# Attention scores on one core: the first unit loaded contiguously and stored in halves of 64 partitions, PSUM in groups of two, three and three banks

## The chip, the core and the metric

The kernel runs on one core of a Trainium2 chip. The metric is the device time in microseconds, the median of several runs. Six names recur. PE is the matrix engine, PEld its loading of weights. DVE is the vector engine, ACT the scalar engine, POOL the general engine GpSimd, and SP the engine that issues most DMAs and waits for their semaphores. All DMAs of a core, whoever issues them, run on its 16 DMA engines.

## The reference

For each of 8 batches and 8 heads, the scores of 512 queries against 512 keys of 64 numbers are computed and scaled. There is no softmax, so the output is much larger than the inputs: 67.1 MB of float32 against twice 8.4 MB.

```python
# q, k: (8, 8, 512, 64) float32
scale = 1.0 / np.sqrt(q.shape[-1])
return (np.einsum('bhqd,bhkd->bhqk', q, k) * scale).astype(np.float32)
```

## The kernel before

**Units and tiles.** The work is cut into 4 units of two batches each (index `v`), and the output into 16 tiles of 4 MB (index `g`), four for each unit. A tile holds four heads: two (`x`) lie one behind the other in each partition, and two (`h`) in partitions 0 to 63 and 64 to 127. A partition holds 8 rows (`i`) of 512 scores for each `x`. Two successive tiles belong to the same batch `b`.

**Loads.** `rows(v, x)` gives the DRAM view of the keys (`x` = 0) or queries (`x` = 1) of one unit: 128 partitions of 16 KB, in the order (s h m) (b x), where the head number is split as (x s h). This order makes the two heads in the halves of a tile neighbours in DRAM, so that a whole tile is one regular pattern over 128 partitions (`out_r`). The loads go to the three large buffers `bigs`, which later hold the tiles on their way out. The keys of unit 0 are loaded in four parts by `load_part` (line 78): part `n` fills every fourth partition, 32 partitions in all, 512 KB. Part 0 goes out on SP's queue and part 1 on ACT's before the program's first barrier, parts 2 and 3 on SP after it. The other loads are 2 MB each, on SP (`load`, line 70). The last two wait until unit 1 has been cast, since they reuse its buffer.

**Cast and transpose.** POOL casts each load to bf16 into `xb` (line 131), in two instructions per load, and counts `ready`. For unit 0's keys it waits for all four parts first. DVE then transposes 32x32 blocks: for each batch two instructions for the keys into `kT` (`turn_keys`, line 162) and four for the queries into `qz` (`turn_queries`, line 170). `qz` is zeroed once (line 185), so that one matmul handles two heads: the rows that belong to the other head are zero. The transposes of the next batch are put in between the evacuations of the present one, at places that a table fixes:

```python
after = {(0, 1): 1, (0, 4): 1, (0, 6): 2, (1, 1): 2}
```

**Matmuls and PSUM.** PE runs 16 matmuls of 128x512 per tile (line 152), in a hardware loop over four tiles. PSUM has 8 banks, used as four tensors `pss` of two banks. A pair of matmuls fills one of them; PE waits until the pair four places earlier has been read.

**Evacuation.** Each pair is scaled and moved to the tile's buffer by ACT (line 202) or DVE (line 205), one instruction of 128x1024 each, in an order written out by hand:

```python
takers = ["act", "dve", "act", "act", "dve", "act", "dve", "act"]
```

So a tile takes five instructions on ACT and three on DVE. Each one counts a semaphore `act0`, `act1`, `dve0` or `dve1` (by batch, alternating).

**Stores and buffers.** SP waits until both counters say that tile `g` is complete (line 102), issues its store as one DMA (line 103), and then waits until the buffer of tile `g + 2` is free: until the store that used it has landed, or, at the start, until POOL has cast what was loaded there (line 112). It then counts `next0` or `next1`, for which PE waits before it begins that tile. Everything on SP is in this one order. After the last store it waits for all stores to land (line 114).

Of the kernel before, what the change touches and what calls it, by code (L numbers as in the profile page):

```python
# [5 lines left out]
def kernel(  # L6
# [5 lines left out]
    nc = tc.nc  # L12
    B, H, S, D = q.shape
    scale = 1.0 / (D ** 0.5)
    P = 128
    Q = 32
    UNITS = B // 2
    G = H // 2
    M = P // (2 * H)
    R = S // M  # L20
    J = R // 2
    RO = 8
    U = S // RO
    JJ = J // RO
    PAIRS = RO
    ALL = 2 * B

    f32 = mybir.dt.float32
    bf16 = mybir.dt.bfloat16
    mult = mybir.AluOpType.mult  # L30
# [3 lines left out]
    names = ["ready", "zeroed", "pe", "next0", "next1", "act0", "act1", "dve0", "dve1"]  # L34
    sem = {name: nc.alloc_semaphore(name) for name in names}
    load_sems = [nc.alloc_semaphore(f"load{n}") for n in range(2 * UNITS)]
    parts = [load_sems[0]] + [nc.alloc_semaphore(f"load0_{n}") for n in range(1, 4)]
    store_sems = [nc.alloc_semaphore(f"store{n}") for n in range(3)]

    q_r = q.rearrange("(v b) (x s h) (m j) d -> v (s h m) (b x) (j d)", b=2, x=2, s=2, j=R)
    k_r = k.rearrange("(v b) (x s h) (m j) d -> v (s h m) (b x) (j d)", b=2, x=2, s=2, j=R)
    out_r = out.rearrange("(v b) (x s h) (u i) k -> v s b (h u) x (i k)", b=2, x=2, s=2, i=RO)

    bigs = [nc.alloc_sbuf_tensor(f"big{n}", [P, 2, RO, S], f32)[:] for n in range(3)]
    xb = nc.alloc_sbuf_tensor("xb", [P, 2 * UNITS, J, D, 2], bf16)[:]
    kT = nc.alloc_sbuf_tensor("kT", [P, 2 * G, S], bf16)[:]
    qz = nc.alloc_sbuf_tensor("qz", [P, 2 * G, RO, P], bf16)[:]
    pss = [nc.alloc_psum_tensor(f"ps{n}", [P, 2, S], f32)[:] for n in range(4)]  # L50

    xw = xb.rearrange("p n w d e -> p n (w d e)").bitcast(f32).rearrange(
        "p n (w d) -> p n w d", d=D)
# [5 lines left out]
    def xf(v):  # L59
        return bigs[(0, 1, 2, 1)[v]].rearrange("p x i k -> p (x i k)").rearrange(  # L60
            "p (x s c) -> p x s c", x=2, s=2)

    def store_buffer(g):
        return bigs[(0, 2, 1)[g % 3]]

    def rows(v, x):
        return (k_r, q_r)[x][v]

    def load(v, x):
        nc.sync.dma_start(out=xf(v)[:, x].rearrange("p s c -> p (s c)"), in_=rows(v, x)  # L70
                          ).then_inc(load_sems[2 * v + x], 16)

    def load_part(queue, n):
        dst = xf(0)[:, 0].rearrange("p s c -> p (s c)")[n:P:4]
        return queue.dma_start(out=dst, in_=rows(0, 0)[:, n]).then_inc(parts[n], 16)  # L78

    for n, queue in enumerate((nc.sync, nc.scalar)):  # L80
        tc.no_tile_sem_insts.add(load_part(queue, n).ins.name)
    tc.close()
    tc.compile()  # L83

    takers = ["act", "dve", "act", "act", "dve", "act", "dve", "act"]
    share = {who: takers.count(who) for who in ("act", "dve")}
    taken = [takers[:p + 1].count(takers[p]) for p in range(PAIRS)]


    for n in (2, 3):
        load_part(nc.sync, n)
    for n in range(1, 2 * (UNITS - 1)):
        load(n // 2, n % 2)
    nc.sync.sem_inc(sem["next0"], 1)
# [3 lines left out]
    for g in range(ALL):  # L100
        for who in ("act", "dve"):
            nc.sync.wait_ge(sem[f"{who}{g // 2 % 2}"], share[who] * (g % 2 + 1))
        nc.sync.dma_start(out=out_r[g // 4, g // 2 % 2, g % 2],
                          in_=store_buffer(g).rearrange("p x i k -> p x (i k)")
                          ).then_inc(store_sems[g % 3], 16)
        for later in ((1, 2) if g == 0 else (g + 2,)):
            if later < ALL:
                if later < 3:
                    nc.sync.wait_ge(sem["ready"], 4 + 2 * later)
                else:  # L110
                    nc.sync.wait_ge(store_sems[later % 3], later // 3 * 16)
                nc.sync.sem_inc(sem[f"next{later // 2 % 2}"], 1)  # L112
    for n in range(3):
        nc.sync.wait_ge(store_sems[n], 16 * len(range(n, ALL, 3)))


    for v in range(UNITS):
        for x in range(2):
            for part in [load_sems[2 * v + x]] if v or x else parts:
                nc.gpsimd.wait_ge(part, 16)  # L120
            for s in range(2):
                src = xf(v)[:, x, s]
                dst = xb[:, 2 * v + x]
                if x == 0:
                    src = src.rearrange("p (w e d) -> p w e d", e=2, d=D)
                    dst = dst[:, s * J // 2:(s + 1) * J // 2].rearrange("p w d e -> p w e d")
                else:
                    src = src.rearrange("p (jj e i d) -> p jj e i d", e=2, i=RO, d=D)
                    dst = dst.rearrange("p (i jj) d e -> p jj e i d", i=RO)[
                        :, s * JJ // 2:(s + 1) * JJ // 2]  # L130
                cast = nc.gpsimd.tensor_copy(out=dst, in_=src)  # L131
            cast.then_inc(sem["ready"], 1)

    pe = nc.tensor
    pe.wait_ge(sem["zeroed"], 2)
    with pe.Fori(0, ALL // 4):
        for t in range(4):
            two, r = divmod(t, 2)  # L140
            off = {1: ("act", 2 * share["act"]), 2: ("dve", 2 * share["dve"]), 3: ("next", 2)}
            for p in range(PAIRS):
                n, i = t * 2 + p // 4, p % 4 * 2
                ahead = (p + 4) % PAIRS
                of = t if p >= 4 else (t + 3) % 4
                for w in range(2):
                    if w == 0:
                        who = takers[ahead]
                        pe.wait_ge(sem[f"{who}{of // 2}"], of % 2 * share[who] + taken[ahead])
                    elif p == 0:  # L150
                        pe.wait_ge(sem[f"next{two}"], r + 1)
                    ins = pe.matmul(out=pss[p % 4][:, w, :], lhsT=qz[:, n, i + w], rhs=kT[:, n],  # L152
                                    start=True, stop=True)
                    if w == 0 and r == 1 and p in off:
                        ins.then_inc(sem[f"{off[p][0]}{1 - two}"], -off[p][1])
                ins.then_inc(sem["pe"], 1)

    def turn_keys(b, y):  # L160
        s = b % 2 * 2 * Q
        return nc.vector.transpose(  # L162
            out=kw[2 * y * Q:2 * (y + 1) * Q, b % 2 * G:(b % 2 + 1) * G].rearrange(
                "d g (m w) -> d w m g", w=J),
            in_=xw[s:s + 2 * Q, b // 2 * 2, :, y * Q:(y + 1) * Q])

    def turn_queries(b, y, h):
        s = (b % 2 * 2 + h) * Q
        d = (2 * y + h) * Q
        return nc.vector.transpose(  # L170
            out=qw[d:d + Q, b % 2 * G:(b % 2 + 1) * G, :, h * Q:(h + 1) * Q].rearrange(
                "d g i (m jj) -> d i jj m g", jj=JJ),
            in_=xw[s:s + Q, b // 2 * 2 + 1, :, y * Q:(y + 1) * Q].rearrange(
                "p (i jj) d -> p i jj d", i=RO))

    def steps(b):
        nc.vector.wait_ge(sem["ready"], b // 2 * 2 + 1)
        yield turn_keys(b, 0)
        yield turn_keys(b, 1)
        nc.vector.wait_ge(sem["ready"], b // 2 * 2 + 2)  # L180
        for y in range(2):
            for h in range(2):
                yield turn_queries(b, y, h)
# [7 lines left out]
    last.then_inc(sem["zeroed"], 1)  # L191


    after = {(0, 1): 1, (0, 4): 1, (0, 6): 2, (1, 1): 2}
    coming = iter(())
    for pair in range(ALL * PAIRS):
        g, p = divmod(pair, PAIRS)
        o = store_buffer(g)[:, p // 4, p % 4 * 2:p % 4 * 2 + 2, :]
        ps = pss[pair % 4]
        if takers[p] == "act":  # L200
            nc.scalar.wait_ge(sem["pe"], pair + 1)
            freed = nc.scalar.mul(out=o, in_=ps, mul=scale)  # L202
        else:
            nc.vector.wait_ge(sem["pe"], pair + 1)
            freed = nc.vector.tensor_scalar(out=o, in0=ps, scalar1=scale, scalar2=None, op0=mult)  # L205
        freed.then_inc(sem[f"{takers[p]}{g // 2 % 2}"], 1)
        if p == 0 and g % 2 == 0 and g // 2 + 1 < 2 * UNITS:
            coming = steps(g // 2 + 1)
        for _ in range(after.get((g % 2, p), 0)):
            next(coming, None)  # L210


# [28 lines left out]
```

## Time and profile before

| | |
|---|---|
| median of 3 runs | 201.52 us (201.32 to 201.67) |
| the profiled execution: time, span | 201.43 us, 200.1 us |
| DMA | 83.90 MB (read 16.78, written 67.11), mean 419 GB/s |
| DVE busy | 154.9 us (77%), 97 instructions |
| ACT busy | 79.5 us (40%), 81 instructions |
| PE busy | 85.8 us (43%) |
| POOL busy | 39.0 us (19%), 20 instructions |
| granted PE clock, mean | 0.773 |

The span runs from the first to the last instruction of the profiled execution; the 1.3 us between it and the time lie around it. Busy times are sums over a whole span with different stages in it. An engine can be busy for most of a span and still not set its end, if its work is finished before somebody needs it; and DMA engines have no line of their own in the list of busy times but a row in tenths per slice of the span.

### The profile page before, as it was taken

The page shows a single profiled execution, that of the slowest core. Times are in us where ns is not written, and L with a number is a line of the kernel's source. Part 1 is how long each engine was busy: PE and PEld are TensorE (multiplying, and loading weights), DVE is VectorE, ACT ScalarE, POOL GpSimd, SP SyncE. Part 2 cuts the span into 40 slices and gives each one's busy share as a digit, 9 for nine tenths or more (in the row PEclk, how much of TensorE's full clock was granted, in tenths as well). Part 3 has the DMA queues.
Part 4 walks back from the last instruction along what each step waited for, and adds up shares of the span by engine and source line. Part 5 has one row for each costly group of instructions (what it writes and reads, how often), then busy time and mean ns, then how long its engine had stood idle before and what let it go on. Part 6 is the DMA issues. An engine that isn't in the chain of part 4 may idle for free.

```text
span 200.1 us, 839 instructions
## 1 busy us (share of the span) xinstructions
PE 85.8 (43%) x252; PEld 27.5 (14%) x256; DVE 154.9 (77%) x97; ACT 79.5 (40%) x81; POOL 39.0 (19%) x20
## 2 busy tenths in 40 slices
PE   0000056294844483547236822754575357910000
PEld 0000021121211121112112211211121112300000
DVE  3317959997999899999998999899989996830000
ACT  2000027163752485248443843383437345840000
POOL 0199999996000000000000000000000000000000
PEclk9999999757875588587975799696559667995555
DMA  5999999999999999999999999999999999999996
GB/s 213 380 432 419 432 439 436 423 406 439 429 429 429 436 429 431 426 436 436 429 426 431 436 432 429 429 432 432 429 436 429 432 429 429 426 429 426 436 432 265
DMA packets 5554, 83.90 MB, mean 419 GB/s; under 512 B 432, under 2 KB 432, under 8 KB 432
## 3 DMA queue, kind: packets, MB, share of 16 engines
q1 hardware_dynamic: 5504, 83.36, 97.9%
q10 hardware_dynamic: 48, 0.52, 0.7%
q14 instruction: 2, 0.02, 0.0%
HBM read 16.78 MB, written 67.11 MB: 419 GB/s over the span
## 4 chain that ended last, share of the span: by engine, by line
DVE 54%; DMA 11%; POOL 10%; PE 6%; ACT 3%; SPq 2%; issue 1%
DVE qz L170 24%; DVE big L205 19%; DVE kT L162 12%; DMA big<-in_k_dram 11%; POOL xb L131 10%; PE ps L152 6%; ACT big L202 3%; SPq L70 2%; SPq L78 1%; SPq L112 0%
## 5 line engine op out<-in xcount | busy, mean ns | idle before, releaser
L152 PE MATMUL ps<-kT,qz 128*128 128x512 bf16 x252 | 85.8, 496 | 90.4 <-DVE big L205 57.0
L202 ACT ACTIVATE big<-ps 128x1024 f32<-128x1024 f32 x80 | 78.2, 1025 | 95.4 <-PE ps L152 95.4
L170 DVE STREAM_TRANSPOSE qz<-xb 32x1024 f32<-32x1024 f32 x32 | 64.1, 2004 | 1.5 <-POOL xb L131 1.0
L205 DVE TENSOR_SCALAR big<-ps 128x1024 f32<-128x1024 f32 x48 | 57.8, 1219 | 9.3 <-PE ps L152 8.9
L152 PEld LDWEIGHTS ps<-kT,qz 128*128 128x128 bf16 x256 | 27.5, 118 | 148.3 <-issue 71.6
L131 POOL CAST xb<-big 128x2048 bf16<-128x2048 f32 x16 | 38.8, 2472 | 9.0 <-DMA big<-in_k_dram 8.7
L162 DVE STREAM_TRANSPOSE kT<-xb 64x1024 f32<-64x1024 f32 x16 | 31.1, 1944 | 7.6 <-POOL xb L131 7.1
L185 DVE MEMSET qz<- 128x4096 uint32 x1 | 3.5, 3472 | 3.5 <-PEq L83 3.5
L202 ACT ACT_TABLE_LOAD x1 | 1.3, 1283 | 2.6 <-PEq L83 2.6
L225 POOL MEMSET const-float32-0.0<- 128x1 f32 x1 | 0.1, 99 | 0.2 <-issue 0.2
L225 POOL MEMSET const-bfloat16-1.0<- 128x1 bf16 x1 | 0.1, 102 | 0.0
L225 POOL MEMSET const-uint8-127<- 128x1 uint8 x1 | 0.1, 102 | 0.0
L225 POOL MEMSET const-float32-1.0<- 128x1 f32 x1 | 0.1, 99 | 0.0
## 6 DMA issues: line engine op xcount, KB each, us to landing
out_dram<-big SPq DMA_DIRECT2D x16, 4096.0 KB, 15.0
big<-in_q_dram SPq DMA_DIRECT2D x4, 2048.0 KB, 16.0
big<-in_k_dram SPq DMA_DIRECT2D x3, 2048.0 KB, 14.7
big<-in_k_dram SPq DMA_DIRECT2D x3, 512.0 KB, 5.2
big<-in_k_dram ACTq DMA_DIRECT2D x1, 512.0 KB, 5.7
```

Source lines behind the costliest of these rows:

```text
L70: nc.sync.dma_start(out=xf(v)[:, x].rearrange("p s c -> p (s c)"), in_=rows(v, x)).then_inc(load_sems[2 * v + x], 16)
L78: return queue.dma_start(out=dst, in_=rows(0, 0)[:, n]).then_inc(parts[n], 16)
L131: cast = nc.gpsimd.tensor_copy(out=dst, in_=src)
L152: ins = pe.matmul(out=pss[p % 4][:, w, :], lhsT=qz[:, n, i + w], rhs=kT[:, n], start=True, stop=True)
L162: return nc.vector.transpose(out=kw[2 * y * Q:2 * (y + 1) * Q, b % 2 * G:(b % 2 + 1) * G].rearrange("d g (m w) -> d w m g", w=J), in_=xw[s ...
L170: return nc.vector.transpose(out=qw[d:d + Q, b % 2 * G:(b % 2 + 1) * G, :, h * Q:(h + 1) * Q].rearrange("d g i (m jj) -> d i jj m g", jj=J ...
L185: nc.vector.memset(qz, 0.0).then_inc(sem["zeroed"], 1)
L202: freed = nc.scalar.mul(out=o, in_=ps, mul=scale)
L205: freed = nc.vector.tensor_scalar(out=o, in0=ps, scalar1=scale, scalar2=None, op0=mult)
L225: nc = _bacc.Bacc("TRN2", target_bir_lowering=False, num_devices=1)
```

## The change

Two things change together.

*Unit 0.* The keys and queries of the first two batches are loaded in DRAM order: partition (b, g, m), 16 KB each, 2 MB in one stretch. The first load, of the keys, is cut by columns instead of partitions: two DMAs of 128 partitions with 8 KB each, one on SP's queue and one on ACT's (semaphores `halves`). POOL waits for each half ahead of the cast that reads it. With this order the two heads in the halves of a tile are no longer neighbours but four heads apart, so each of the tiles 0 to 3 is stored by two DMAs, one from partitions 0 to 63 and one from 64 to 127 (`out_0`), and the waits for their buffers count 32 instead of 16 (`stored`). The transposes of batches 0 and 1 put their blocks down in the order (g m) instead of (m g) (`inside`).

*PSUM.* The eight banks are one tensor `ps`, in groups of two, three and three banks. For each half tile (`x`), DVE takes the first group (128x1024), and ACT the other two (128x1536 each). A tile then takes four instructions on ACT and two on DVE. PE waits ahead of the first matmul of each group until the same group of the half tile before has been read. The transposes of the next batch stand two at a time behind DVE's evacuations, in three of every four half tiles.

```diff
-    parts = [load_sems[0]] + [nc.alloc_semaphore(f"load0_{n}") for n in range(1, 4)]
+    halves = [load_sems[0], nc.alloc_semaphore("load0b")]
...
+    out_0 = out.rearrange("b (h t x) (u i) k -> b t h u x (i k)", h=2, x=2, i=RO)
...
-    pss = [nc.alloc_psum_tensor(f"ps{n}", [P, 2, S], f32)[:] for n in range(4)]
+    ps = nc.alloc_psum_tensor("ps", [P, RO, S], f32)[:]
...
     def rows(v, x):
-        return (k_r, q_r)[x][v]
+        if v == 0:
+            return (k, q)[x][:2].rearrange("b g (m j) d -> (b g m) (j d)", j=R)
+        return (k, q)[x].rearrange(
+            "(v b) (x s h) (m j) d -> v (s h m) (b x) (j d)", b=2, x=2, s=2, j=R)[v]
...
-    def load_part(queue, n):
-        dst = xf(0)[:, 0].rearrange("p s c -> p (s c)")[n:P:4]
-        return queue.dma_start(out=dst, in_=rows(0, 0)[:, n]).then_inc(parts[n], 16)
-
-    for n, queue in enumerate((nc.sync, nc.scalar)):
-        tc.no_tile_sem_insts.add(load_part(queue, n).ins.name)
+    for s, queue in enumerate((nc.sync, nc.scalar)):
+        first_load = queue.dma_start(
+            out=xf(0)[:, 0, s], in_=rows(0, 0)[:, s * R * D // 2:(s + 1) * R * D // 2]
+        ).then_inc(halves[s], 16)
+        tc.no_tile_sem_insts.add(first_load.ins.name)
...
-    takers = ["act", "dve", "act", "act", "dve", "act", "dve", "act"]
+    groups = [(0, 2, "dve"), (2, 3, "act"), (5, 3, "act")]
+    share = {"act": 4, "dve": 2}
+
+    def stored(n, tiles):
+        return sum(32 if g < 4 else 16 for g in range(n, tiles, 3))
...
-    for n in (2, 3):
-        load_part(nc.sync, n)
...
-        nc.sync.dma_start(out=out_r[g // 4, g // 2 % 2, g % 2],
-                          in_=store_buffer(g).rearrange("p x i k -> p x (i k)")
-                          ).then_inc(store_sems[g % 3], 16)
+        o = store_buffer(g).rearrange("p x i k -> p x (i k)")
+        if g < 4:
+            for h in range(2):
+                nc.sync.dma_start(out=out_0[g // 2, g % 2, h], in_=o[h * U:(h + 1) * U]
+                                  ).then_inc(store_sems[g % 3], 16)
+        else:
+            nc.sync.dma_start(out=out_r[g // 4, g // 2 % 2, g % 2], in_=o
+                              ).then_inc(store_sems[g % 3], 16)
...
-            for part in [load_sems[2 * v + x]] if v or x else parts:
-                nc.gpsimd.wait_ge(part, 16)
+            if v or x:
+                nc.gpsimd.wait_ge(load_sems[2 * v + x], 16)
             for s in range(2):
+                if v == x == 0:
+                    nc.gpsimd.wait_ge(halves[s], 16)
...
+            for x in range(2):
+                before = (2 * t + x - 1) % 8
+                for i in range(RO):
+                    if i in waits:
+                        who, count = waits[i]
+                        pe.wait_ge(sem[f"{who}{before // 4}"], before % 4 * per_half[who] + count)
+                    elif x == 0 and i == 1:
                         pe.wait_ge(sem[f"next{two}"], r + 1)
-                    ins = pe.matmul(out=pss[p % 4][:, w, :], lhsT=qz[:, n, i + w], rhs=kT[:, n],
+                    ins = pe.matmul(out=ps[:, i], lhsT=qz[:, 2 * t + x, i], rhs=kT[:, 2 * t + x],
                                     start=True, stop=True)
...
+    def inside(b):
+        return "g m" if b < 2 else "m g"
...
-                "d g (m w) -> d w m g", w=J),
+                f"d g (m w) -> d w {inside(b)}", w=J),
...
-    after = {(0, 1): 1, (0, 4): 1, (0, 6): 2, (1, 1): 2}
...
+            for i, rows_, who in groups:
+                count += 1
+                engine = nc.scalar if who == "act" else nc.vector
+                engine.wait_ge(sem["pe"], count)
+                o, src = store_buffer(g)[:, x, i:i + rows_], ps[:, i:i + rows_]
...
+            for _ in range(2 if (g % 2, x) != (1, 1) else 0):
+                next(coming, None)
```

More of the change, by code (lines that the diff above doesn't have):

```diff
@@ L24 @@
     JJ = J // RO
-    PAIRS = RO
     ALL = 2 * B
@@ L36 @@
     load_sems = [nc.alloc_semaphore(f"load{n}") for n in range(2 * UNITS)]
-    parts = [load_sems[0]] + [nc.alloc_semaphore(f"load0_{n}") for n in range(1, 4)]
+    halves = [load_sems[0], nc.alloc_semaphore("load0b")]
     store_sems = [nc.alloc_semaphore(f"store{n}") for n in range(3)]
-    q_r = q.rearrange("(v b) (x s h) (m j) d -> v (s h m) (b x) (j d)", b=2, x=2, s=2, j=R)
-    k_r = k.rearrange("(v b) (x s h) (m j) d -> v (s h m) (b x) (j d)", b=2, x=2, s=2, j=R)
+    out_0 = out.rearrange("b (h t x) (u i) k -> b t h u x (i k)", h=2, x=2, i=RO)
     out_r = out.rearrange("(v b) (x s h) (u i) k -> v s b (h u) x (i k)", b=2, x=2, s=2, i=RO)
@@ L71, in load @@
                           ).then_inc(load_sems[2 * v + x], 16)
-    def load_part(queue, n):
-        dst = xf(0)[:, 0].rearrange("p s c -> p (s c)")[n:P:4]
-        return queue.dma_start(out=dst, in_=rows(0, 0)[:, n]).then_inc(parts[n], 16)
-    for n, queue in enumerate((nc.sync, nc.scalar)):
-        tc.no_tile_sem_insts.add(load_part(queue, n).ins.name)
+    for s, queue in enumerate((nc.sync, nc.scalar)):
[3 more added lines that the diff above has]
+        tc.no_tile_sem_insts.add(first_load.ins.name)
     tc.close()
     tc.compile()
-    takers = ["act", "dve", "act", "act", "dve", "act", "dve", "act"]
-    share = {who: takers.count(who) for who in ("act", "dve")}
-    taken = [takers[:p + 1].count(takers[p]) for p in range(PAIRS)]
-    for n in (2, 3):
-        load_part(nc.sync, n)
+    groups = [(0, 2, "dve"), (2, 3, "act"), (5, 3, "act")]
+    share = {"act": 4, "dve": 2}
+    def stored(n, tiles):
+        return sum(32 if g < 4 else 16 for g in range(n, tiles, 3))
     for n in range(1, 2 * (UNITS - 1)):
@@ L110 @@
                 else:
-                    nc.sync.wait_ge(store_sems[later % 3], later // 3 * 16)
+                    nc.sync.wait_ge(store_sems[later % 3], stored(later % 3, later))
                 nc.sync.sem_inc(sem[f"next{later // 2 % 2}"], 1)
     for n in range(3):
-        nc.sync.wait_ge(store_sems[n], 16 * len(range(n, ALL, 3)))
+        nc.sync.wait_ge(store_sems[n], stored(n, ALL))
     for v in range(UNITS):
         for x in range(2):
-            for part in [load_sems[2 * v + x]] if v or x else parts:
-                nc.gpsimd.wait_ge(part, 16)
+            if v or x:
+                nc.gpsimd.wait_ge(load_sems[2 * v + x], 16)
             for s in range(2):
+                if v == x == 0:
+                    nc.gpsimd.wait_ge(halves[s], 16)
                 src = xf(v)[:, x, s]
@@ L136 @@
     pe = nc.tensor
+    waits, signals = {}, []
+    for i, rows_, who in groups:
+        waits[i] = (who, [w for _, _, w in groups[:groups.index((i, rows_, who)) + 1]].count(who))
+        signals.append(i + rows_ - 1)
+    per_half = {who: count // 2 for who, count in share.items()}
+    takes = {(0, 3): ("next", 2), (1, 3): ("dve", 2 * share["dve"]), (1, 6): ("act", 2 * share["act"])}
     pe.wait_ge(sem["zeroed"], 2)
@@ L140 @@
             two, r = divmod(t, 2)
[L141 to L150, printed above, removed]
+            for x in range(2):
[5 more added lines that the diff above has]
+                    elif x == 0 and i == 1:
                         pe.wait_ge(sem[f"next{two}"], r + 1)
-                    ins = pe.matmul(out=pss[p % 4][:, w, :], lhsT=qz[:, n, i + w], rhs=kT[:, n],
+                    ins = pe.matmul(out=ps[:, i], lhsT=qz[:, 2 * t + x, i], rhs=kT[:, 2 * t + x],
                                     start=True, stop=True)
-                    if w == 0 and r == 1 and p in off:
-                        ins.then_inc(sem[f"{off[p][0]}{1 - two}"], -off[p][1])
-                ins.then_inc(sem["pe"], 1)
+                    if i in signals:
+                        ins.then_inc(sem["pe"], 1)
+                    elif r == 1 and (x, i) in takes:
+                        name, count = takes[x, i]
+                        ins.then_inc(sem[f"{name}{1 - two}"], -count)
+    def inside(b):
+        return "g m" if b < 2 else "m g"
     def turn_keys(b, y):
@@ L171, in turn_queries @@
             out=qw[d:d + Q, b % 2 * G:(b % 2 + 1) * G, :, h * Q:(h + 1) * Q].rearrange(
-                "d g i (m jj) -> d i jj m g", jj=JJ),
+                f"d g i (m jj) -> d i jj {inside(b)}", jj=JJ),
             in_=xw[s:s + Q, b // 2 * 2 + 1, :, y * Q:(y + 1) * Q].rearrange(
@@ L191 @@
     last.then_inc(sem["zeroed"], 1)
-    after = {(0, 1): 1, (0, 4): 1, (0, 6): 2, (1, 1): 2}
     coming = iter(())
[L196 to L210, printed above, removed]
+    count = 0
+    for g in range(ALL):
+        for x in range(2):
+            for i, rows_, who in groups:
+                count += 1
+                engine = nc.scalar if who == "act" else nc.vector
+                engine.wait_ge(sem["pe"], count)
+                o, src = store_buffer(g)[:, x, i:i + rows_], ps[:, i:i + rows_]
+                if who == "act":
+                    freed = engine.mul(out=o, in_=src, mul=scale)
+                else:
+                    freed = engine.tensor_scalar(out=o, in0=src, scalar1=scale, scalar2=None,
+                                                 op0=mult)
+                freed.then_inc(sem[f"{who}{g // 2 % 2}"], 1)
+            if x == 0 and g % 2 == 0 and g // 2 + 1 < 2 * UNITS:
+                coming = steps(g // 2 + 1)
+            for _ in range(2 if (g % 2, x) != (1, 1) else 0):
+                next(coming, None)
 _INS = ['q', 'k']
```

## The prediction

> **What bounds the kernel now.** I read the slices of the span first, because 83.90 MB have to pass and the question is whether any other engine ever makes the transfers stop.
>
> ```profile
> span 200.1 us, 839 instructions
> PE 85.8 (43%) x252; PEld 27.5 (14%) x256; DVE 154.9 (77%) x97; ACT 79.5 (40%) x81; POOL 39.0 (19%) x20
> ...
> DMA  5999999999999999999999999999999999999996
> ...
> DMA packets 5554, 83.90 MB, mean 419 GB/s; under 512 B 432, under 2 KB 432, under 8 KB 432
> ```
>
> The DMA row is 9 in every slice but the first and the last. So the 16 DMA engines work without a pause from 2 us on, and the time is bytes over rate. DVE, at 77%, looks busiest among the compute engines, but its work only has to be early enough. The stretches of the span, with the busy times of PE, PEld, DVE, ACT and POOL, then clock, DMA share and GB/s, show where the rate is lost:
>
> ```profile
> 2.00:10.00 8.00, 0.00 (x0) 0.00 (x0) 3.47 (x1) 1.28 (x1) 0.89 (x1) 1.00 0.98 371
> ...
> 3.00:5.00 2.00, 0.00 (x0) 0.00 (x0) 1.53 (x1) 0.83 (x1) 0.00 (x0) 1.00 1.00 393
> 5.00:7.00 2.00, 0.00 (x0) 0.00 (x0) 1.95 (x1) 0.00 (x0) 0.00 (x0) 1.00 1.01 369
> ...
> 44.00:100.00 56.00, 30.79 (x91) 9.61 (x91) 53.37 (x35) 28.98 (x30) 4.28 (x2) 0.75 1.01 431
> 100.00:160.00 60.00, 31.78 (x95) 10.34 (x96) 56.95 (x38) 29.44 (x30) 0.00 (x0) 0.75 1.01 431
> ```
>
> From 44 us on 431 GB/s: a tile of 4.194 MB takes 4.194/0.431 = 9.73 us. From 2 to 10 us only 371: 8 x (431 - 371) = 0.48 MB are missing, 1.1 us of DMA time. That, and the tail after 197 us, is all the DMA loses. The waits of the store queue on SP and the issues say how much room compute leaves:
>
> ```profile
> SPq L102 <- DVE big L205: 75.1, 16, 7.5
> SPq L112 <- DMA out_dram<-big: 54.0, 13, 5.4
> ...
> out_dram<-big SPq DMA_DIRECT2D x16, 4096.0 KB, 15.0
> ```
>
> A store lands 15.0 us after its issue but needs 9.73 us, so some 5 us of stores normally stand queued. SP's wait of 75.1 us for DVE is therefore not idle DMA. The costs that the change touches are in these groups:
>
> ```profile
> L202 ACT ACTIVATE big<-ps 128x1024 f32<-128x1024 f32 x80 | 78.2, 1025 | 95.4 <-PE ps L152 95.4
> L170 DVE STREAM_TRANSPOSE qz<-xb 32x1024 f32<-32x1024 f32 x32 | 64.1, 2004 | 1.5 <-POOL xb L131 1.0
> L205 DVE TENSOR_SCALAR big<-ps 128x1024 f32<-128x1024 f32 x48 | 57.8, 1219 | 9.3 <-PE ps L152 8.9
> ...
> L162 DVE STREAM_TRANSPOSE kT<-xb 64x1024 f32<-64x1024 f32 x16 | 31.1, 1944 | 7.6 <-POOL xb L131 7.1
> ```
>
> [...]
>
> **The change part by part.**
>
> *First load.* Four loads of 32 partitions (512 KB; three on SP, one on ACT) become two of 128 partitions with 8 KB each (1 MB; one on SP, one on ACT). The bytes are the same 2 MB. SP loses two issues of about 0.56 us ahead of the q load, whose own issue took 1.68 us at 3.72 us, so SP's next loads are queued about 1.2 us sooner, while 2.1/0.431 = 4.9 us of first-load work is already queued. POOL casts the first half as soon as it lands, instead of after all four parts. Of the 1.1 us lost from 2 to 10 us, the ramp of the first packets (0.9 us at 309 GB/s, (431 - 309) x 0.9 / 431 = 0.25 us) stays. Bounds for the gain: 0.85 us if all else goes, and -0.3 us if 8 KB pieces start more slowly than 16 KB ones. I take 0.6 us. DMA is the bound, so it counts in full.
>
> *Stores of tiles 0 to 3.* Four stores become eight, of 64 partitions each. SP issues four more, 4 x 0.37 us, beside 15 us of queued work: nothing. What is queued behind them on SP are the buffer releases (the adds to next0 and next1), 0.4 us later, again inside the wait for a store. Tiles 3 to 6 wait for both halves of the store three tiles earlier, and these now end together or one behind the other, at the same total. Their rate is the open cost. At 431 GB/s it is 4 x 9.73 = 38.9 us as now, cost 0. [...] Below nothing there is no room, since 431 is the rate of everything else.
>
> I take 0, with little lead, for a reason in the trace. The first-load parts have 32 partitions, every fourth one. [...] While those parts pass, the trace has 393 and 369. [...]
>
> *Transposes of unit 0.* 12 of 48 write with another order inside (32 equal steps instead of 8 by 4). No row shows that form; the same element count takes 1.94 and 2.00 us, which I take: 0. Cover: tile 0's store is issued at 36.9 us and the last load lands at about 43.4 (issued 28.7, 14.7 us), so 6.5 us. Six of the twelve stand before the first matmul; 1 us more each would be hidden, double the time would open a gap of 12 - 6.5 = 5.5 us, and a faster form gains nothing.
>
> *Evacuation.* DVE does 32 instead of 48 of 1024 columns, ACT 64 of 1536 instead of 80 of 1024. Per two tiles DVE has 4 x 1.22 + 2 x 1.94 + 4 x 2.00 = 16.8 us instead of 19.2; [...] two tiles of stores take 19.5. So DVE, which is nearly level with the stores now, comes free by 2.4 us per pair. It buys nothing, because the DMA is already full. The added coupling: the first matmul of a half tile waits for DVE, behind two transposes (4 us), and both ACT groups are queued behind it on PE. A half is then 1.22 + 4.0 = 5.2 us on DVE[...]. In the half without transposes DVE waits for two matmuls, some 0.9 us. That makes 17.7 us per pair, under 19.5: 0. If the pair came to 20.5 us, six pairs would cost 6 us, of which the early tile and the queued 5 us hide nearly all.
>
> Sum: 201.43 (profiled execution; span 200.1 and 1.3 around it) - 0.6 = 200.8. The median of the runs is 201.52, 0.09 above the profiled one: **200.9**.
>
> **Rivals.**
> 1. [...] Mechanism: tiles 0 to 3, from about 43 us; [...] and the second half comes behind the first. [...] It decides as soon as the four tiles are over 1.5% slower (0.6 of 38.9 us). [...] Against it: the rate of the parts. Compute could not shorten it: it would wait for buffers.
> 2. *Sharing in part.* Engines drift apart, so that some are on the second half while others are on the first; or a half costs only its own start and end. Between +2 and +28 us: 203 to 229. Bigger ACT groups that let the queue run dry at the start would also end here, at the low edge.
> 3. *Nothing changes.* The early loss is HBM's and not that of the small parts; 201.4. For it: in 7 to 9 us, when the q load passes too, the rate is also low (352).
>
> **How the numbers follow.** A measurement of this kernel can tell about 0.2%, 0.4 us, from no change. Full rate has 0.50: in it 0.27 for faster than that, 0.18 for within (rival 3 and a small gain), 0.05 for a slower start or a small loss at the seams. Rival 1 has 0.36, rival 2 has 0.14, both slower. That sums to 0.27, 0.18 and 0.55. The likeliest case's own range is 200.2 to 202.2. The range has to reach the half-rate case[...]: I end it at 241.
>
> **What would show it.** In the stretches, 2 to 10 us should come to about 405 GB/s instead of 371, and 44 to 83 us should stay at 431; half rate would show there as about 215 with tile 0 to 3 stores landing 30 us or more after issue, and SP waiting for stores instead of for DVE. Busy DVE should fall to about 32 x 1.22 + 95.2 + 3.5 = 138 us[...]. I am wrong in the working if compute, and not the rate of stores, opens a gap in the DMA row.

## The result, and the profile after

| | before | after |
|---|---|---|
| median | 201.53 us (201.32 to 202.29, 6 runs) | 235.76 us (231.84 to 237.6, 6 runs) |
| ratio after / before | | 1.158 (95% interval 1.148 to 1.168) |
| profiled execution: time, span | 201.43 us, 200.1 us | 235.71 us, 234.4 us |
| DVE busy, ACT busy | 154.9, 79.5 us | 137.1, 89.8 us |

The runs after scatter by 2.5%, far more than those before; the ratio is taken over the two of them that lie within 1.5% of the fastest, which puts the loss at 32 us, while the median of all six and the profiled execution put it at 34. Rows of the page after, in slices of 234.4/40 = 5.9 us:

```profile
span 234.4 us, 783 instructions
...
DVE  5068798779640592550099969959959992140000
...
DMA  6999999999999999999999999999999999999970
GB/s 232 442 428 431 431 428 422 338 227 201 249 249 221 249 288 266 246 280 274 369 424 419 433 428 431 425 426 431 431 419 436 419 431 422 431 428 422 428 327 39
```

But for its two ends, the DMA row is what it was: busy everywhere. The row below it is not. From the ninth slice to the nineteenth the DMA engines, as busy as ever, move only 201 to 288 GB/s. A busy share alone would have hidden this. DVE has gaps of whole slices there (the zeros), so it waits for others. The same stretch more closely, with busy times of PE, PEld, DVE, ACT and POOL, then clock, DMA share and GB/s:

```profile
2.00:10.00 8.00, 0.00 (x0) 0.00 (x0) 3.47 (x1) 1.20 (x1) 1.39 (x1) 1.00 0.97 389
...
44.00:50.00 6.00, 2.59 (x7) 0.92 (x8) 2.77 (x4) 1.72 (x3) 3.71 (x2) 0.82 1.05 243
50.00:60.00 10.00, 3.46 (x12) 1.03 (x12) 8.69 (x5) 5.20 (x4) 0.00 (x0) 0.84 0.97 224
60.00:70.00 10.00, 5.84 (x15) 1.89 (x16) 6.46 (x4) 5.58 (x4) 0.00 (x0) 0.67 1.04 244
70.00:80.00 10.00, 1.84 (x5) 0.74 (x6) 1.19 (x1) 0.00 (x0) 0.00 (x0) 0.50 0.98 239
80.00:90.00 10.00, 4.01 (x13) 1.08 (x10) 9.01 (x6) 5.54 (x4) 0.00 (x0) 0.84 1.00 247
90.00:100.00 10.00, 4.52 (x12) 1.50 (x12) 3.86 (x3) 2.63 (x2) 0.00 (x0) 0.55 0.98 277
100.00:110.00 10.00, 1.21 (x4) 0.31 (x4) 2.64 (x2) 2.85 (x3) 0.00 (x0) 0.79 1.01 267
110.00:120.00 10.00, 2.97 (x8) 1.05 (x9) 2.30 (x2) 1.05 (x1) 0.00 (x0) 0.50 0.95 375
120.00:226.00 106.00, 55.36 (x150) 17.72 (x151) 69.33 (x43) 54.37 (x40) 0.00 (x0) 0.73 1.01 427
226.00:234.00 8.00, 0.00 (x0) 0.00 (x0) 0.00 (x0) 0.00 (x0) 0.00 (x0) 0.50 0.21 90
```

The tail of the kernel before, for comparison:

```profile
197.00:200.10 3.10, 0.00 (x0) 0.00 (x0) 0.00 (x0) 0.00 (x0) 0.00 (x0) 0.50 0.40 169
```

These rows account for the whole loss of this execution. From 44 to 120 us 20.2 MB pass instead of 0.431 x 76 = 32.8 MB: 12.6 MB, or 29.2 us of DMA time. In the last 8 us 0.72 MB pass instead of 3.45, 6.3 us; before, the tail lost 1.9, so 4.4 us are new. From 120 to 226 us the rate is 427 instead of 431, 1.0 us. Going the other way, 2 to 10 us now has 389 GB/s instead of 371, 0.3 us. The sum is 29.2 + 4.4 + 1.0 - 0.3 = 34.3 us, and the spans differ by 34.3.

The waits of SP turn round as well. Before, it waited mostly for DVE to complete a tile (75.1 us); now it waits for stores to land, so that buffers come free:

```profile
SPq L117 <- DMA out_dram<-big: 142.2, 13, 21.0
...
SPq L102 <- DVE big L221: 10.0, 2, 5.4
```

By itself this turn is no sign of slow stores: a run below with the new PSUM groups and whole stores shows it too, at 201.16 us.

The groups and the issues of the page after:

```profile
L219 ACT ACTIVATE big<-ps 128x1536 f32<-128x1536 f32 x64 | 88.5, 1452 | 120.7 <-PE ps L162 120.7
L221 DVE TENSOR_SCALAR big<-ps 128x1024 f32<-128x1024 f32 x32 | 39.2, 1225 | 61.0 <-PE ps L162 53.2
L185 DVE STREAM_TRANSPOSE qz<-xb 32x1024 f32<-32x1024 f32 x32 | 63.8, 1994 | 1.4 <-POOL xb L138 1.0
...
L177 DVE STREAM_TRANSPOSE kT<-xb 64x1024 f32<-64x1024 f32 x16 | 31.2, 1950 | 7.6 <-POOL xb L138 7.2
...
out_dram<-big SPq DMA_DIRECT2D x12, 4096.0 KB, 19.5
out_dram<-big SPq DMA_DIRECT2D x8, 2048.0 KB, 26.1
```

DVE's instructions took what they took before: 1225, 1994 and 1950 ns, against 1219, 2004 and 1944. A half-store of 2 MB takes longer to land (26.1 us) than a whole one of 4 MB did before (15.0 us).

### The profile page after: what moved, and what is told of

Read it like the earlier page. It is cut to its first block, busy times and chain, and to the rows that moved or that the text cites. A ratio compares the mean times of both kernels' runs of the same rounds, so it can differ in the third digit from the quotient of the medians.

```text
span 234.4 us, 783 instructions
## 1 busy us (share of the span) xinstructions
PE 93.1 (40%) x252; PEld 29.8 (13%) x256; DVE 137.1 (58%) x81; ACT 89.8 (38%) x65; POOL 39.0 (17%) x20
## 3 DMA queue, kind: packets, MB, share of 16 engines
q10 hardware_dynamic: 144, 1.05, 1.1%
## 4 chain that ended last, share of the span: by engine, by line
DMA 77%; ACT 5%; DVE 3%; POOL 2%; PE 2%; issue 1%; SPq 1%; DVEq 0%
DMA out_dram<-big 72%; DMA big<-in_q_dram 5%; ACT big L219 5%; DVE qz L185 3%; POOL xb L138 2%; PE ps L162 2%; SPq L106 1%; SPq L117 0%; SPq L102 0%; DVEq L195 0%
## 5 line engine op out<-in xcount | busy, mean ns | idle before, releaser
L162 PE MATMUL ps<-kT,qz 128*128 128x512 bf16 x252 | 93.1, 531 | 117.5 <-SPq L117 65.8
L219 ACT ACTIVATE big<-ps 128x1536 f32<-128x1536 f32 x64 | 88.5, 1452 | 120.7 <-PE ps L162 120.7
L221 DVE TENSOR_SCALAR big<-ps 128x1024 f32<-128x1024 f32 x32 | 39.2, 1225 | 61.0 <-PE ps L162 53.2
L185 DVE STREAM_TRANSPOSE qz<-xb 32x1024 f32<-32x1024 f32 x32 | 63.8, 1994 | 1.4 <-POOL xb L138 1.0
L162 PEld LDWEIGHTS ps<-kT,qz 128*128 128x128 bf16 x256 | 29.8, 126 | 180.3 <-SPq L117 69.0
L177 DVE STREAM_TRANSPOSE kT<-xb 64x1024 f32<-64x1024 f32 x16 | 31.2, 1950 | 7.6 <-POOL xb L138 7.2
## 6 DMA issues: line engine op xcount, KB each, us to landing
out_dram<-big SPq DMA_DIRECT2D x8, 2048.0 KB, 26.1
```

The lines of the kernel that those rows point to most:

```text
L162: ins = pe.matmul(out=ps[:, i], lhsT=qz[:, 2 * t + x, i], rhs=kT[:, 2 * t + x], start=True, stop=True)
L177: return nc.vector.transpose(out=kw[2 * y * Q:2 * (y + 1) * Q, b % 2 * G:(b % 2 + 1) * G].rearrange(f"d g (m w) -> d w {inside(b)}", w=J), ...
L185: return nc.vector.transpose(out=qw[d:d + Q, b % 2 * G:(b % 2 + 1) * G, :, h * Q:(h + 1) * Q].rearrange(f"d g i (m jj) -> d i jj {inside(b ...
L219: freed = engine.mul(out=o, in_=src, mul=scale)
L221: freed = engine.tensor_scalar(out=o, in0=src, scalar1=scale, scalar2=None, op0=mult)
```

## The experiments

**Which edit costs it.** Three theories were open. P, which is rival 1 of the prediction, and which no trace of the kernel before shows, as it has no such store: a store from one half of the partitions passes at about half the rate. G: the larger PSUM groups hold compute back. D: the two halves of a tile now lie four heads apart in DRAM, and that is slow. The first run takes the PSUM part of the change alone, with unit 0 loaded, transposed and stored as before. One line of that part:

```diff
+    groups = [(0, 2, "dve"), (2, 3, "act"), (5, 3, "act")]
```

> The PSUM groups of two, three and three alone; unit 0 is loaded and stored as before. Theory P [...]: no such store is left, so 201.5 us, within 0.5 of before, with DVE busy near 137 us. Rival G (the larger groups hold PE and ACT back, and the added time is compute): most of the added 34 us comes back, 225 to 236.

Measured: 201.36 us, ratio 0.9992 (0.9983 to 1.0002), DVE busy 137.6 us. G is out as the cause of the loss: 17 us less of DVE work and 11 us more of ACT work change nothing that can be measured. The second run adds only the half-stores to the kernel before, so that the halves are neighbours in DRAM:

```diff
+        dst = out_r[g // 4, g // 2 % 2, g % 2]
+        if g < 4:
+            for n in range(2):
+                nc.sync.dma_start(out=dst[n * U:(n + 1) * U], in_=o[n * U:(n + 1) * U]).then_inc(store_sems[g % 3], 16)
```

> The kernel before with one edit: tiles 0 to 3 are stored by two stores of 64 partitions each; layout, loads and PSUM as before. Theory P: nearly the whole loss of the change, 230 to 238 us, and about 217 to 245 GB/s while the four tiles are stored. Rival D (the contiguous unit 0 writes its two halves four heads apart in DRAM, and that is slow): here the two halves are neighbours in DRAM, so 201.5. Rival G: 201.5.

Measured: 235.62 us, ratio 1.165 (1.163 to 1.168). This one edit is the whole loss, and D is out. The stretches of its profiled execution (238.5 us) show the same low rates, 231 to 244 GB/s:

```profile
50.00:60.00 10.00, 4.27 (x12) 1.32 (x10) 9.91 (x7) 4.22 (x5) 0.00 (x0) 0.67 1.00 231
60.00:70.00 10.00, 6.65 (x16) 2.25 (x16) 8.47 (x6) 5.01 (x5) 0.00 (x0) 0.66 1.02 242
70.00:80.00 10.00, 0.54 (x2) 0.27 (x3) 0.05 (x1) 0.00 (x0) 0.00 (x0) 0.51 1.01 244
```

**What about the half-stores costs it.** They are more in number, they have 64 partitions, and their partitions are adjacent. Two runs take these apart, again on the kernel before; their diffs are shown against the edit just above. The first cuts the tile by `x`:

```diff
-                nc.sync.dma_start(out=dst[n * U:(n + 1) * U], in_=o[n * U:(n + 1) * U])
+                nc.sync.dma_start(out=dst[:, n], in_=o[:, n])
```

> The kernel before with tiles 0 to 3 stored by two stores each that both take all 128 partitions, one head x each (2 MB, as many stores as with halves). Theory P: [...] 201.5 us within 0.5. Rival N (it is the number of stores and their fixed cost, and two at a time can't overlap): as slow as with halves of the partitions, 230 or more.

Measured: 201.59 us, ratio 1.0007 (1.0000 to 1.0015). Twice as many stores, each over all partitions, cost at most 0.3 us. This run answers a rival on the side of DRAM as well: by the access patterns, its eight stores write the same eight stretches of 2 MB (heads 0 and 1, 2 and 3, and so on, of batches 0 and 1) as the half-stores of the changed kernel, in the same pieces of 16 KB. What differs is the partitions that the data come from, and the order of the tiles: in the kernel before two successive tiles are the same four heads of two batches, and not, as its description above has it, tiles of one batch. The second takes every second partition:

```diff
-                nc.sync.dma_start(out=dst[n * U:(n + 1) * U], in_=o[n * U:(n + 1) * U])
+                nc.sync.dma_start(out=dst[n:P:2], in_=o[n:P:2])
```

> The kernel before with tiles 0 to 3 stored by two stores of every second partition: 64 partitions each, but spread over both halves[...]. Theory P[...]: 201.5 us. Theory P [...] the time is between 201.5 and 236[...]. Rival W (it is the 64 partitions of a store, wherever they lie): 230 or more.

Measured: 201.74 us, ratio 1.0010 (0.9996 to 1.0024). 64 partitions are no handicap if they are spread. The stretches of this run while tiles 0 to 3 are stored:

```profile
44.00:54.00 10.00, 5.17 (x17) 1.76 (x16) 8.21 (x6) 4.63 (x6) 5.11 (x3) 0.83 1.00 426
54.00:64.00 10.00, 3.68 (x14) 1.01 (x14) 9.90 (x8) 4.66 (x5) 0.00 (x0) 0.78 1.02 436
64.00:74.00 10.00, 7.44 (x21) 2.40 (x20) 9.88 (x7) 5.41 (x6) 0.00 (x0) 0.71 1.00 428
```

Full rate from the first tile on, 426 to 436 GB/s. So it is where the 64 partitions lie, as theory P has it.

**Packets at half speed.** The traces keep more than these views show: start and duration of every packet that a DMA engine moves. All stores here go in packets of 16 KB. In the kernel before, all 262 packets that start between 50 and 60 us take 0.61 to 0.63 us, and so do all that start from 44 to 64 us in the run with every second partition (at most 0.64). In the changed kernel, from 50 to 60 us, the typical packet takes 1.27 us, twice as long, and only 13% take the single time (under 0.66 us). The DMA share is 0.97 in these 10 us, so the engines are at work nearly all the time, and most packets take twice as long. One would see this if the engines took turns in pairs. That is my supposition, made from the doubling alone; the trace shows the doubling, and neither pairs nor anything that they share.

**Why not 39 us, and why the long tail.** Four tiles at half of the 431 GB/s would cost 4 x 9.73 = 38.9 us more (an estimate from the rate before). The change cost 34 in the profiled execution, the rate rises from 224 to 277 GB/s while the tiles pass, and at the end the DMA engines don't stop together. One more supposition would explain all three, called the drift below: the engines fall apart from tile to tile, and two engines no longer slow each other down once one is at the second half-store while the other is still at the first.

The same trace has two signs of this. The packets of the single time become more, from 13% of those that start between 50 and 60 us to 48% between 90 and 100 us, while the median of the others is still 1.27 us: slow packets don't become faster, they become fewer. And the lead can be seen. Each store raises its semaphore in 16 counts, whose times are kept; I read them as one from each engine. From the first to the last count of a half-store pass 0.6 us at first and then, from one to the next, 1.4, 1.8, 2.6, 3.4, 4.1 and 4.8 us. At the eighth, the last before a whole tile, it is 11.6. The whole stores after it close nothing: from tile 5 on the counts of each lie about 8 us apart, and those of the last come from 226.5 to 234.3 us. That is the long tail; in the kernel before the last counts lie 1.7 us apart. Whether two engines make a pair, and which, the trace doesn't tell.

Three runs change the number of such stores (`g < 1`, `g < 16`) or their size. The first:

> The kernel before with tile 0 alone stored by two stores of 64 partitions. Fixed half rate: [...] Drift [...]: at the first tile they are still together, so also 210 to 211, and no long tail. If the loss were a start-up cost of the first such store: as much as with four tiles, 235.

Measured: 210.34 us, ratio 1.044 (1.042 to 1.046), +9.0 us. One tile pays nearly the full price of half rate, 9.7 us. A smaller lead stays, and with it there is no long tail: the last counts lie 3.1 us apart, the last 3 us move 186 GB/s, and before, the last 3.1 us moved 169.

```profile
44.00:54.00 10.00, 6.40 (x20) 2.03 (x18) 8.53 (x7) 5.85 (x7) 4.64 (x2) 0.80 1.00 238
54.00:62.00 8.00, 0.39 (x1) 0.10 (x1) 7.47 (x5) 0.85 (x1) 0.00 (x0) 0.76 0.98 246
62.00:84.00 22.00, 13.64 (x36) 4.79 (x38) 17.73 (x12) 10.83 (x11) 0.00 (x0) 0.73 1.01 429
...
206.00:209.00 3.00, 0.00 (x0) 0.00 (x0) 0.00 (x0) 0.00 (x0) 0.00 (x0) 0.50 0.44 186
```

> The kernel before with all 16 tiles stored by two stores of 64 partitions. Fixed half rate: [...] Drift: after some four tiles the engines of a pair are half a tile apart, [...] and the rest passes at about 430 GB/s; 235 to 245 us, hardly more than with four tiles.

Measured: 269.1 us as the median of four runs between 246.1 and 283.2; with such a scatter no ratio is given. A fixed half rate (201.4 + 16 x 9.73 = 357 us, an estimate from the 431 GB/s) is out by far, and all four runs lie above my 235 to 245: the slowing fades, but does not end. The stretches of the profiled run (271.7 us) show how far it gets:

```profile
44.00:64.00 20.00, 8.89 (x25) 3.28 (x27) 17.54 (x13) 7.70 (x9) 4.44 (x2) 0.79 1.01 237
...
84.00:104.00 20.00, 5.96 (x17) 2.03 (x16) 14.03 (x10) 6.23 (x7) 0.00 (x0) 0.73 1.00 275
...
124.00:144.00 20.00, 8.37 (x23) 3.13 (x25) 10.25 (x8) 6.81 (x7) 0.00 (x0) 0.67 0.99 349
...
164.00:184.00 20.00, 11.36 (x30) 4.01 (x31) 17.56 (x11) 9.91 (x10) 0.00 (x0) 0.72 1.00 364
184.00:204.00 20.00, 8.90 (x22) 3.08 (x23) 13.03 (x10) 6.04 (x6) 0.00 (x0) 0.62 0.97 329
```

From 237 the rate climbs to 364 and then falls again, with busy engines in all these stretches. The packets go with it: 16% take the single time from 50 to 60 us, 80% from 160 to 190 us, and 52% from 230 to 240 us. But the lead is not lost: the counts of the last half-store lie 14.3 us apart. One reading would fit both. A half-store is 128 packets of 16 KB, 8 for each of 16 engines if they are dealt out evenly, and 8 x 0.61 = 4.9 us at the single time. Then a lead of that size would part a pair, and a lead of two half-stores, 9.8 us (both estimates from these packets), would bring it together again. That is not shown, since pairs can't be seen, and what makes the lead grow is open.

The third run cuts the stores in four, in the order low, high, low, high partitions:

```diff
+                p0 = (0, 64, 32, 96)[n]
+                nc.sync.dma_start(out=dst[p0:p0 + 32], in_=o[p0:p0 + 32]).then_inc(store_sems[g % 3], 16)
```

> The kernel before with tiles 0 to 3 stored by four stores of 32 partitions each, in the order 0 to 31, 64 to 95, 32 to 63, 96 to 127, so that low and high partitions alternate twice as often. Fixed half rate: 235 to 239 us[...]. Drift: an engine needs only half the lead[...], so about half of the loss, 212 to 222 us. [...]

Measured: 216.5 us, ratio 1.075 (1.071 to 1.079), +15 us. Each of these stores still lies in one half of the partitions, so a rate fixed by the store's own half would have given the 235 of the halves. With half the lead to gain, somewhat under half the loss is left, as the drift would have it. Its rate is 280, 329 and 406 GB/s in the three stretches of 10 us from 44 us on.

**Two queues.** In the changed kernel, the second half of tiles 0 to 3 is issued by ACT, behind waits for the tile's counters:

```diff
-            for h in range(2):
-                nc.sync.dma_start(out=out_0[g // 2, g % 2, h], in_=o[h * U:(h + 1) * U]
+            nc.sync.dma_start(out=out_0[g // 2, g % 2, 0], in_=o[:U]).then_inc(store_sems[g % 3], 16)
...
+            nc.scalar.dma_start(
+                out=out_0[g // 2, g % 2, 1],
```

> The changed kernel with one edit: of the tiles 0 to 3, the second half (partitions 64 to 127) is issued on ACT's queue instead of SP's. [...] If engines take turns between the two queues: a lead of one packet is enough for a pair to fall apart, and the time is 201 to 207 us. If the second queue waits for the first (or the pairs stay in step): 232 to 239 as now.

Measured: 212.2 us, ratio 1.056 (1.050 to 1.061). Neither expectation hit. By the ratios, 11 of the 32 us are left, so the second queue does not simply wait, but full rate does not come back either:

```profile
54.00:64.00 10.00, 5.73 (x18) 1.80 (x18) 9.92 (x7) 7.07 (x6) 0.00 (x0) 0.84 1.03 354
64.00:74.00 10.00, 7.82 (x23) 2.44 (x20) 8.59 (x6) 5.94 (x5) 0.00 (x0) 0.70 0.98 352
74.00:84.00 10.00, 3.48 (x10) 1.11 (x9) 7.98 (x6) 3.35 (x3) 0.00 (x0) 0.64 1.00 347
```

The rate stays near 350, and 72% of the packets that start in these 30 us take the single time. How the engines choose between the queues was not tried further.

**Is it DMA time alone?** In the changed kernel, tiles also wait for buffers. With the half-stores at the last four tiles (`g >= 12`), nothing later is left to wait.

> The kernel before with tiles 12 to 15, the last four, stored by two stores of 64 partitions each; no later tile waits for a buffer then. If the loss is DMA time alone: as much as with tiles 0 to 3, 230 to 240 us. If a part of it is compute that waits for buffers which come free late: clearly less, 215 to 228.

Measured: 232.1 us, ratio 1.152 (1.150 to 1.154). By the ratio that is +30.5 us, against +33.2 with tiles 0 to 3 on the same kernel. Three of its stretches:

```profile
165.00:175.00 10.00, 5.68 (x17) 1.86 (x17) 6.38 (x6) 4.79 (x5) 0.00 (x0) 0.83 1.01 220
...
215.00:225.00 10.00, 0.00 (x0) 0.00 (x0) 0.00 (x0) 0.00 (x0) 0.00 (x0) 0.50 1.01 264
225.00:231.00 6.00, 0.00 (x0) 0.00 (x0) 0.00 (x0) 0.00 (x0) 0.00 (x0) 0.50 0.49 142
```

From 195 us on no compute engine works, so no store waits for a tile, and yet the rate stays at 247 to 277 GB/s until 225 us, with a DMA share near 1. So most of the loss is DMA time, wherever the tiles stand. Whether the other 2.7 us are waiting for buffers or another course of the drift (its last counts lie 6.2 us apart) is open.

**The other half of the change, the first load.** Two runs cut the first load by columns, as the change does, but keep the order of partitions that allows whole stores: one with the pairs of before, one with the groups of the change.

```diff
+            out=xf(0)[:, 0, s], in_=rows(0, 0)[:, :, s * R * D // 2:(s + 1) * R * D // 2]
```

> The kernel before with one edit: the first load cut by columns into two loads of 128 partitions, one on SP and one on ACT, instead of four parts of 32 partitions; PSUM pairs and everything else as before. If the early loss belongs to the small parts: 200.9 to 201.2. If it is HBM's: 201.4, as before.

Measured: 201.40 us, ratio 0.9998 (0.9989 to 1.0006): nothing.

> The good parts of the change put together: PSUM groups of two, three and three; the first load cut by columns into two loads of 128 partitions with 8 KB each, one on SP and one on ACT; but the order of partitions of unit 0 as before, so that every tile is one store of 128 partitions. Theory P: no half-store is left, so the transfers run at 430 throughout, and of the start-up loss some 0.5 us comes back: 200.9 to 201.2. If the start-up gain seen in the changed kernel (its q load of unit 0 landed about 0.6 us sooner) needs the contiguous order in DRAM: 201.4.

Measured: 201.16 us, ratio 0.9986 (0.9977 to 0.9995). It is the fastest of all, by 0.3 us, which is under what I had called tellable (0.4 us); with 13 runs the interval just leaves 1 out. Its waits of SP are the ones announced above:

```profile
SPq L115 <- DMA out_dram<-big: 108.6, 13, 9.3
...
SPq L100 <- DVE big L219: 17.1, 6, 5.6
```

With the new groups compute completes its tiles earlier, and SP waits for stores although these run at full rate. Where the start-up gain went is in the stretches of the first of these two runs, with pairs:

```profile
2.00:10.00 8.00, 0.00 (x0) 0.00 (x0) 3.47 (x1) 1.28 (x1) 2.45 (x1) 1.00 1.00 393
...
38.00:44.00 6.00, 5.00 (x15) 1.53 (x13) 5.93 (x5) 4.70 (x5) 5.05 (x3) 0.72 1.03 385
```

and in the same late stretch of the kernel before:

```profile
38.00:44.00 6.00, 5.41 (x13) 1.95 (x14) 5.94 (x4) 3.46 (x4) 5.95 (x4) 0.50 1.01 415
```

Early, 8 x (393 - 371) = 176 KB more have passed. From 38 to 44 us, where the last load ends and the first store begins, 6 x (415 - 385) = 180 KB fewer pass. In this run the gain is given back in full. What slows the transfers there is open.

## Why the prediction was wrong

**The step that failed** is the rate of the stores of tiles 0 to 3: "I take 0, with little lead". The term measured +32 to +34 us in place of 0. While the first three tiles pass, the rate is 224 to 247 GB/s in place of 431; that this is a little above half, 215.5, would fit the drift.

The 0 was carried over from the first load: parts of 32 spread partitions had run at 393 and 369 GB/s, so half-stores were to run at about the full rate too. What joined the two was my assumption on how partitions and DMA engines go together, which no trace shows. The run with every second partition, at 426 to 436 GB/s, shows that spread partitions can run at full rate. But that says nothing on adjacent ones. The changed kernel's stretches refute the 0: the DMA share is about 1 at 240 GB/s, and the typical packet takes 1.27 us instead of 0.61. That engines slow each other down in pairs remains a supposition: neither pairs nor how the partitions are dealt out to the engines is shown.

Nor was the observation as clean as it was taken to be. The 393 and 369 are below 431, and of the packets that start from 3 to 9 us in the kernel before, 26% take over 0.66 us, up to 1.35. With the first load cut by columns it is 2% (in the run with pairs). So the spread parts did have slowed packets, though far fewer than the half-stores; whether the cause is the same is not shown. The evidence for the 0 came from a case that differs in just the property in question, adjacency.

**Rival 1**, half rate for each half-store, came nearest. At half of 431 GB/s the time would be 201.4 + 38.9 - 0.6 = 239.7 us (an estimate from the rate before), 4 us above the median, because the slowing fades. For one tile the same estimate is good: 9.7 us, and 9.0 measured. The drift was named in rival 2, but as an alternative to rival 1 and not as something that could go on in it. Its range for that, up to 229 us, was too low. That a lead comes back as a tail (4.4 us) was not foreseen.

**The first load**: 0.6 us was expected, with 405 GB/s from 2 to 10 us. The changed kernel has 389, worth 0.3 us: it starts more slowly, with 164 and 311 GB/s in the third and fourth us, and is at full rate from 4 us on. In the run where it stands alone it is worth nothing, since it is given back at 38 to 44 us. So the number of rival 3 came, 201.4 us, but not for its reason: without the small parts the early rate did rise, from 371 to 393. The step left out that a gain at the start of a saturated queue has to survive every later change from loads to stores.

**What held**: the evacuation at 0, shown by itself (ratio 0.9992). DVE busy was expected at 138 us and is 137.1; ACT rose from 79.5 to 89.8. Its instruction takes 1452 ns for 1536 columns, and 1025 for 1024 before; instructions overlap a little (64 x 1452 ns would be 92.9 us, and the group shows 88.5). The transposes in the other order cost the same, 1950 and 1994 ns. Four more issues on SP cost nothing, though each took 0.65 us and not 0.37: as many stores over all partitions took 0.1 us more. Of the signs to look for, the low rate came (224 to 247 where 215 was named), and late landings in part (26.1 us in the median, 38.1 at most, where 30 or more was named). SP waiting for stores came too, but it was a poor sign, since the PSUM groups alone bring it about.

## What to carry to other kernels

When a tile is stored in pieces, cut it so that every piece spreads over the whole range of partitions: by columns, or every second partition. Two pieces from partitions 0 to 63 and 64 to 127, one behind the other on one queue, begin at about half rate (224 to 247 GB/s here, where whole tiles pass at 431), and issuing both does not join them. Loads into one half of the partitions were not tried. Before a layout is changed for the sake of a load, ask what its stores will look like: here 0.3 us at the start was bought with over 30 us later. And read GB/s beside the busy share, because slow packets count as busy time: here a share of 0.97 to 1.05 stood beside 224 to 247 GB/s.

## What the runs showed of the hardware that was not expected

- A store from 64 adjacent partitions makes single packets slow, and not all of them: most 16 KB packets took 1.27 us instead of 0.61. With every second partition none took over 0.64 us from 44 to 64 us.
- This is not a fixed half rate. One tile in halves costs 9.0 us, four cost 34, sixteen 68 instead of 156 (16 x 9.73), with runs from 246 to 283 us.
- The lead within a store lasts to the end: after four half-stored tiles near the start, the counts of every whole store from tile 5 on lay about 8 us apart, and the last 8 us of the span moved 90 GB/s, at a DMA share of 0.21.
- The two halves on two queues ran at about 350 GB/s, on one queue at about 240.
